# Six units by token halves behind each norm, weight remainders on GpSimd, and a later second layer, in a two-layer hybrid transformer

## The chip, the cores and the metric

The kernel runs on one core of a Trainium2 chip. A core has TensorE (PE) for matmuls, VectorE (DVE), ScalarE (ACT), GpSimd (POOL) and SyncE (SP); each runs its own instructions in a fixed order and waits for the others by semaphores. Matmuls write to PSUM, which has eight banks here. The metric is the device time of one launch in microseconds (us).

## The reference

Two layers over 512 tokens of width 1024, in fp32. Each layer has a mixer of four branches and a convolutional FFN, each between two RMS norms:

```python
for l in range(DEPTH):                       # 2
    h = rms_norm(x, norm_mix_pre[l])
    z = h @ w_in[l]
    za, zq, zkv, zg, zc, zd = jnp.split(z, offsets, axis=-1)
    y_conv = conformer_conv(za, ...)         # 31 taps per channel
    y_nsa = nsa_attention(q, kv..., gates, nsa_pe_k[l], nsa_pe_v[l],
                          nsa_ck_w1[l], nsa_ck_w2[l], nsa_cv_w1[l], nsa_cv_w2[l], cos, sin)
    y_sgu = spatial_gating(zc, ...)
    y_pool = multiscale_pool(zd, ...)
    y = jnp.concatenate([y_conv, y_nsa, y_sgu, y_pool], axis=-1) @ w_out[l]
    x = x + rms_norm(y, norm_mix_post[l])
    h = rms_norm(x, norm_ffn_pre[l])
    y = conv_ffn(h, ffn_up[l], ffn_conv_w[l], ffn_conv_b[l], ffn_down[l])   # 1024 -> 5632 -> 1024
    x = x + rms_norm(y, norm_ffn_post[l])

def compress(t, pe, w1, w2):                 # in nsa_attention, for keys and for values
    blocks = (t[:, blk_idx] + pe).reshape(bsz, n_cmp, CMP_LEN * HEAD_DIM)
    return jax.nn.gelu(blocks @ w1) @ w2     # first layer, gelu, second layer
```

## The kernel before, in words

Activations lie with channels on the 128 partitions and tokens along the free dimension (512, or two token halves of 256). A weight matrix is cut into units of 128 output columns, 92 per layer: four of NAT (tables that are wanted with tokens on the partitions), KK and CMP (keys, and what the compression reads), two of Q, four of CONV, two of SU (the spatial gating), two of the pooling branch, eight of the output projection, 44 of the FFN's up matrix (from `U_UP` = 24 on) and 24 of its down matrix (three phases of eight).

Each fp32 operand is split in a high part and a remainder, so a product is three matmuls per k-tile: hi x h's high part (`hh`), hi x h's remainder (`hl`), and lo x `hh` (lines L125 to L127). With eight k-tiles a unit is 24 matmuls of 512 columns, or 48 of 256 by token halves. `weights()` (L104 to L114) makes the two parts of a unit: a DMA loads `raw`, ACT copies it to `whi` (rounded to the matmul's type) and writes -`raw`, rounded alike, to `wlo`, and a DMA of POOL's queue reads the weight from HBM a second time and adds it to `wlo`, which leaves the remainder. `whi` and `wlo` have six buffers each, `raw` has two:

```python
nc.scalar.activation(hi[:, :cols], raw[:, :cols], AF.Copy)
nc.scalar.activation(lo[:, :cols], raw[:, :cols], AF.Copy, scale=-1.0)
nc.gpsimd.dma_start(lo[:, :cols], self.a["ws"][l, u, :, :cols], accum_op=OP.add)
```

The rows name these by line: L111 for the hi copy, L112 for the second copy, L113 for the accumulating DMA.

A norm seam works by token halves. `in_halves` computes the last six output tiles of a projection for half 0 and then for half 1, and after each half calls `post_norm`: a matmul with ones sums the squares over partitions (L212, the statistic), ACT takes the root (L213), DVE the reciprocal (L214, into `q` for half 0, `kh` for half 1, `rsx` for the next norm), `z` is scaled (L272), added to `x` by POOL or DVE (L99), and split again into `hh` (ACT, L246) and `hl` (DVE, L247), with squares (L236, L239) and a second statistic for the norm that follows, whose factor `rsx` is applied to the products afterwards. Statistics of half 0 have the PSUM bank "o", of half 1 bank "t" (two buffers, shared with the attention); products rotate through the five banks "mm" and "s". Behind a seam the first units are computed by halves, half 0 of all of them first, so that PE works while half 1 is normed: five up units in `ffn()`, four units (KK, CMP, two Q) in `mixer()`.

The mixer issues its steps from a list, `STEPS`. Among them "cmp" makes the compressed keys and values: the first layer (L497), a gelu on ACT (L502), and the second layer (L504, L510). The 31 taps of the convolution are DVE instructions (L609, L611); a rotary embedding swaps half of the rows by a DMA. In the FFN each up unit passes `conv3` (DVE L99, L809, ACT L806), pairs are gated (ACT L819) and split into `yh` and `yl` (L131, L99), and a phase's down units follow. The order on each engine is fixed when the program is built: a scheduler estimates times and places each instruction, so that a change in one part can move rows in another.

## Time and profile before

| | |
|---|---|
| time, median of 3 runs | 1229.5 us (1229.41 to 1232.96) |
| the profiled execution's time | 1228.64 us |
| its span, first to last instruction | 1226.7 us |
| mean granted TensorE clock | 0.971 |
| busy: PE, DVE, ACT, POOL | 1143.6, 663.1, 705.4, 336.1 us |
| HBM read | 192.79 MB |

Busy time counts an engine's instructions without its waits. The granted clock is a share of 2.4 GHz; 0.5 would be the lower level, 1.2 GHz. In the stretches, each engine has its busy time and its number of instructions, and then follow clock, DMA share and GB/s.

### The profile page before, as it was taken

Reading aid. Unit: us, or ns where it says so; the run is one execution under the profiler, and the core shown is the slowest. Engines: PE = TensorE matmul, PEld = TensorE weight load, DVE = VectorE, ACT = ScalarE, POOL = GpSimd, SP = SyncE. Lnnn points to the kernel's source line nnn. Section 1 sums busy time; section 2 is a strip of 40 time slices with the busy share of each in tenths; the row PEclk is TensorE's granted clock in tenths of the full one; section 3 lists DMA queues with packets and bytes.
Section 4 is the critical chain, followed back from the end, with each engine's and each line's share of the span. In section 5 each row is a group of like instructions: output and inputs, shape, how many; then the busy total and the mean of one; then the engine's idle time right before and its main releaser. Section 6 shows DMA issues by size and latency. Waiting matters only on the chain.

```text
span 1226.7 us, 16283 instructions
## 1 busy us (share of the span) xinstructions
PE 1143.6 (93%) x6168; PEld 956.0 (78%) x6168; DVE 663.1 (54%) x1065; ACT 705.4 (58%) x1094; POOL 336.1 (27%) x378
## 2 busy tenths in 40 slices
PE   6979899879999999999978899987999999999995
PEld 5868568878888888888976776877888888888895
DVE  5689951785125521544678998147550544134536
ACT  6558756567456544565464687554756664446541
POOL 2352642331111111111344545233212111111112
PEclk9989999889999999999989899997999999999998
DMA  8977514748799979887659391083879987889842
GB/s 233 244 174 161 117 52 104 172 119 182 167 238 205 187 182 195 189 186 157 149 123 217 75 205 36 1 202 74 199 154 231 225 187 172 205 186 189 183 96 68
DMA packets 64094, 197.53 MB, mean 161 GB/s; under 512 B 8720, under 2 KB 14864, under 8 KB 64016
## 3 DMA queue, kind: packets, MB, share of 16 engines
q0 software_dynamic: 26352, 92.91, 41.7%
q1 hardware_dynamic: 37664, 103.59, 28.4%
q8 instruction: 48, 0.79, 0.3%
...
HBM read 192.79 MB, written 2.10 MB: 159 GB/s over the span
## 4 chain that ended last, share of the span: by engine, by line
PE 73%; DVE 10%; DMA 6%; ACT 6%; issue 3%; SPq 1%; DVEq 0%; ACTq 0%; POOLq 0%
PE ps_s L126 13%; PE ps_s L127 13%; PE ps_s L125 13%; PE ps_mm L126 9%; PE ps_mm L127 9%; PE ps_mm L125 9%; DVE z L272 3%; DMA raw<-in_ws_dram 2%; DMA wlo<-in_ws_dram 2%; DVE z L611 2%; ACT wlo L112 1%; PE ps_o L742 1%; ACT whi L111 1%; PE ps_t L733 1%; DMA yh<-yh 1%
## 5 line engine op out<-in xcount | busy, mean ns | idle before, releaser
L113 POOL DMA_DIRECT2D wlo<-in_ws_dram x183 | 161.1, 883 | 716.4 <-ACT wlo L112 625.1
L111 ACT ACTIVATE whi<-raw 128x1024 fp32r<-128x1024 f32 (+2 forms) x183 | 188.4, 1030 | 249.1 <-PE ps_s L126 94.4
L126 PE MATMUL ps_s<-hl,whi 128*128 128x512 f32 (+1 forms) x552 | 202.8, 369 | 11.0 <-DVE hl L247 10.9
L125 PE MATMUL ps_s<-hh,whi 128*128 128x512 f32 (+1 forms) x552 | 200.9, 369 | 5.4 <-ACT hh L246 5.2
L127 PE MATMUL ps_s<-hh,wlo 128*128 128x512 f32 (+1 forms) x552 | 202.2, 368 | 2.5 <-DMA wlo<-in_ws_dram 2.5
L125 PE MATMUL ps_mm<-hh,whi 128*128 128x512 f32 (+1 forms) x488 | 184.8, 379 | 12.4 <-ACT hh L246 8.4
L126 PE MATMUL ps_mm<-hl,whi 128*128 128x512 f32 (+1 forms) x488 | 185.9, 381 | 10.9 <-DVE hl L247 10.5
L112 ACT ACTIVATE wlo<-raw 128x1024 fp32r<-128x1024 f32 (+2 forms) x183 | 186.3, 1018 | 0.7 <-PE ps_s L390 0.3
L127 PE MATMUL ps_mm<-hh,wlo 128*128 128x512 f32 (+1 forms) x488 | 184.2, 377 | 0.0
L126 PE MATMUL ps_s<-yl,whi 128*128 128x256 f32 (+1 forms) x406 | 134.9, 333 | 0.0
L127 PE MATMUL ps_s<-yh,wlo 128*128 128x256 f32 (+1 forms) x406 | 134.5, 332 | 0.2 <-DMA wlo<-in_ws_dram 0.2
L125 PE MATMUL ps_s<-yh,whi 128*128 128x256 f32 (+1 forms) x406 | 133.9, 334 | 0.4 <-ACT yh L131 0.3
L126 PEld LDWEIGHTS ps_s<-hl,whi 128*128 128x128 f32 x552 | 108.3, 197 | 29.7 <-DVE hl L247 12.2
L125 PEld LDWEIGHTS ps_s<-hh,whi 128*128 128x128 f32 x552 | 107.2, 197 | 23.6 <-ACT hh L246 5.6
L127 PEld LDWEIGHTS ps_s<-hh,wlo 128*128 128x128 f32 x552 | 108.0, 196 | 20.2 <-DMA wlo<-in_ws_dram 2.7
L125 PEld LDWEIGHTS ps_mm<-hh,whi 128*128 128x128 f32 x488 | 95.3, 195 | 30.7 <-ACT hh L246 9.0
L126 PEld LDWEIGHTS ps_mm<-hl,whi 128*128 128x128 f32 x488 | 95.0, 195 | 30.0 <-DVE hl L247 13.3
L127 PEld LDWEIGHTS ps_mm<-hh,wlo 128*128 128x128 f32 x488 | 95.1, 195 | 17.0
L809 DVE SCALAR_TENSOR_TENSOR q<-q,vec,q 128x511 f32<-128x511 f32 (+1 forms) x88 | 65.5, 750 | 57.3 <-ACT q L806 55.8
L127 PE MATMUL ps_mm<-yh,wlo 128*128 128x256 f32 (+1 forms) x266 | 87.5, 329 | 3.0 <-DMA wlo<-in_ws_dram 3.0
L125 PE MATMUL ps_mm<-yh,whi 128*128 128x256 f32 (+1 forms) x266 | 87.9, 331 | 0.0
L126 PE MATMUL ps_mm<-yl,whi 128*128 128x256 f32 (+1 forms) x266 | 87.4, 329 | 0.0
...
## 6 DMA issues: line engine op xcount, KB each, us to landing
raw<-in_ws_dram SPq DMA_DIRECT2D x159, 512.0 KB, 6.2
wlo<-in_ws_dram POOLq DMA_DIRECT2D x159, 512.0 KB, 7.6
...
```

Of the source, the lines that this page charges most:

```text
L111: nc.scalar.activation(hi[:, :cols], raw[:, :cols], AF.Copy)
L112: nc.scalar.activation(lo[:, :cols], raw[:, :cols], AF.Copy, scale=-1.0)
L113: nc.gpsimd.dma_start(lo[:, :cols], self.a["ws"][l, u, :, :cols], accum_op=OP.add)
L125: nc.tensor.matmul(ps, wh, ah, start=start and n == 0, stop=False)
L126: nc.tensor.matmul(ps, wh, al, start=False, stop=False)
L127: nc.tensor.matmul(ps, wl, ah, start=False, stop=stop and n == len(ks) - 1)
L272: nc.vector.scalar_tensor_tensor(t, t, gain(k), rs, op0=OP.mult, op1=OP.mult)
L611: nc.vector.scalar_tensor_tensor(acc[j], x, w, acc[j], op0=OP.mult, op1=OP.add)
L733: nc.tensor.transpose(pst[:, s * 128:(s + 1) * 128], P[s][:, kb * 128:(kb + 1) * 128], self.ident)
L742: nc.tensor.matmul(O[64 * c:64 * c + 64, :256], v, PT[:, 256 * c:256 * c + 256], start=b == 0 and kb == 0, stop=False, skip_group_check=True)
L809: nc.vector.scalar_tensor_tensor(t[:, s:], v[:, :S - s], fw(k), t[:, s:], op0=OP.mult, op1=OP.add)
```

## The change

It has four parts. (1) Six up units instead of five go by token halves behind a norm, and in the mixer six instead of four: `MORE` adds the two units of the first CONV step. (2) Where these are computed, and for all up units, products rotate through seven PSUM banks (the two of tag "t" join); the statistics of both halves share bank "o". (3) `on_dma(u)` decides how the remainder of a weight is made. Units below `U_UP + 10` keep ACT's second copy and the accumulating DMA, except CMP and Q at the start of the first layer; for these, and for the later 34 up and all 24 down units of each layer, POOL subtracts `whi` from `raw` in two column halves. (4) The second layer of the compression is a step of its own, "cmp2", behind the scores "a1".

```diff
--- before.py
+++ after.py
@@ -67,14 +67,16 @@
 
     LAST_POOL = (1, 4)
 
-    FIRST, FULL = 5, 2
+    FIRST, FULL = 6, 2
+
+    DMA_UPS, AT_START = 10, (U_KK, U_CMP, U_Q, U_Q + 1)
 
     FIRST_CUTS = ((0, 2), (2, 5), (5, 8))
 
     def __init__(self, tc, nc, a, cp, mp, wp, pp):
         self.tc, self.nc, self.a = tc, nc, a
         self.cp, self.mp, self.wp, self.pp = cp, mp, wp, pp
-        self.cyc = 0
+        self.cyc = self.l = 0
         self.fcyc = 0
 
 
@@ -90,16 +92,20 @@
         return self.pp.tile(list(shape), F, name="ps_" + tag, tag=tag,
                             bufs={"s": 3, "t": 2, "o": 1, "mm": 2}[tag])
 
-    def psr(self):
-        tag = ("mm", "s", "mm", "s", "s")[self.cyc % 5]
+    def psr(self, wide=False):
+        tags = ("mm", "s", "t", "mm", "s", "t", "s") if wide else ("mm", "s", "mm", "s", "s")
         self.cyc += 1
-        return self.ps(tag)
+        return self.ps(tags[self.cyc % len(tags)])
 
     def tt(self, out, x, y, op, eng=None):
         (eng or self.nc.vector).tensor_tensor(out, x, y, op=op)
 
     def eng(self, name):
         return self.nc.gpsimd if name in self.ON_POOL else self.nc.vector
+
+    def on_dma(self, u):
+
+        return u < U_UP + self.DMA_UPS and not (self.l == 0 and u in self.AT_START)
 
     def weights(self, l, u, cols=1024):
 
@@ -107,10 +113,16 @@
         raw = self.wp.tile([128, 1024], F, name="raw", tag="raw", bufs=self.RAW_BUFS)
         hi = self.wp.tile([128, 1024], R, name="whi", tag="whi", bufs=self.W_BUFS)
         lo = self.wp.tile([128, 1024], R, name="wlo", tag="wlo", bufs=self.W_BUFS)
-        nc.sync.dma_start(raw[:, :cols], self.a["ws"][l, u, :, :cols])
+        src = self.a["ws"][l, u, :, :cols]
+        nc.sync.dma_start(raw[:, :cols], src)
         nc.scalar.activation(hi[:, :cols], raw[:, :cols], AF.Copy)
-        nc.scalar.activation(lo[:, :cols], raw[:, :cols], AF.Copy, scale=-1.0)
-        nc.gpsimd.dma_start(lo[:, :cols], self.a["ws"][l, u, :, :cols], accum_op=OP.add)
+        if self.on_dma(u):
+            nc.scalar.activation(lo[:, :cols], raw[:, :cols], AF.Copy, scale=-1.0)
+            nc.gpsimd.dma_start(lo[:, :cols], src, accum_op=OP.add)
+        else:
+            n = cols // self.LO_CUT
+            for c in range(0, cols, n):
+                self.tt(lo[:, c:c + n], raw[:, c:c + n], hi[:, c:c + n].bitcast(F), OP.subtract, nc.gpsimd)
         return hi, lo
 
     def product(self, ps, w, ks, act, c0=0, c1=512, start=True, stop=True, kw=None):
@@ -217,7 +229,7 @@
 
         tags = (("q20", "q21", "q22", "q23"), ("kh0", "kh1", "kl0", "kl1"))[c]
         acc, rs = self.slot(tags[0]), self.slot(tags[1])
-        return {"c": slice(256 * c, 256 * c + 256), "tags": tags[2:], "n": 0, "pair": None, "ps": ("o", "t")[c],
+        return {"c": slice(256 * c, 256 * c + 256), "tags": tags[2:], "n": 0, "pair": None, "ps": "o",
                 "acc": [acc[:, :256], acc[:, 256:]], "rs": [rs[:, :256], rs[:, 256:]]}
 
     def pair(self, H):
@@ -339,7 +351,9 @@
     def first_weights(self, l):
         return [self.weights(l, u) for u in (U_KK, U_CMP, U_Q, U_Q + 1)]
 
-    STEPS = ("conv0", "consts", "conv1", "cmp", "kk", "q1", "nat", "w", "q0", "gates", "a1", "taps", "probs", "su",
+
+    MORE = (U_CONV + 2, U_CONV)
+    STEPS = ("conv0", "consts", "conv1", "cmp", "kk", "q1", "nat", "w", "q0", "gates", "a1", "cmp2", "taps", "probs", "su",
              "v", "pool0", "a0", "b0", "b1", "p0", "p1", "pool1", "a2", "b2", "fp", "p2", "a3", "b3", "p3", "fg",
              "others", "sum", "cn")
 
@@ -349,7 +363,9 @@
         h, rsx = self.h, self.rsx
 
         wk = self.first if l == 0 else self.first_weights(l)
-        psk, psc, *psq = pk = [self.psr() for _ in wk]
+        wk = wk + [self.weights(l, u) for u in self.MORE]
+        pk = [self.psr(True) for _ in wk]
+        psk, psc, psq, ahead = pk[0], pk[1], pk[2:4], dict(zip(self.MORE, pk[4:]))
         for c in range(2):
             for ps, w in zip(pk, wk):
                 self.product(ps[:, 256 * c:256 * c + 256], w, range(KT), h, 256 * c, 256 * c + 256)
@@ -359,6 +375,8 @@
         m = {}
 
         def proj(u):
+            if u in ahead:
+                return ahead[u]
             ps = self.ps("mm")
             self.product(ps, self.weights(l, u), range(KT), h)
             return ps
@@ -449,7 +467,8 @@
             m["pcT"] = self.compressed_probs(qc, m["gates"])
 
         steps = {
-            "consts": constants, "nat": nat, "gates": gates, "kk": keys, "cmp": lambda: self.compressed(l, psc), "probs": probs,
+            "consts": constants, "nat": nat, "gates": gates, "kk": keys, "cmp": lambda: m.update(g1=self.compressed(l, psc)),
+            "cmp2": lambda: self.compressed_out(m["g1"]), "probs": probs,
             "su": lambda: self.gating_u([proj(U_SU + j) for j in range(2)]),
             "v": lambda: self.gating_v(m["nat"]), "w": self.gating_w, "fg": lambda: self.gating_finish(m["nat"]),
             "taps": lambda: self.taps(gl, acc), "others": lambda: self.other_taps(gl),
@@ -500,6 +519,11 @@
         nc.vector.tensor_copy(g1, ps1[64:, :64])
         self.tt(g1, g1, ps1[:64, :64], OP.add)
         nc.scalar.activation(g1, g1, AF.Gelu_apprx_tanh)
+        return g1
+
+    def compressed_out(self, g1):
+
+        nc = self.nc
         ps2 = self.ps("o")
         nc.tensor.matmul(ps2[:, :32], self.w2[:, :128], g1[:, :32], start=True, stop=True)
         for p in (0, 64):
@@ -826,7 +850,7 @@
         self.new_z()
         first = self.FIRST
         ws = [self.weights(l, U_UP + m) for m in range(first)]
-        pss = [self.psr() for _ in range(first)]
+        pss = [self.psr(True) for _ in range(first)]
         for c in range(2):
             for m in range(first):
                 self.product(pss[m][:, c * 256:(c + 1) * 256], ws[m], range(KT), h, c * 256, (c + 1) * 256)
@@ -839,7 +863,7 @@
                     if m < first:
                         ps = pss[m]
                     else:
-                        ps = self.psr()
+                        ps = self.psr(True)
                         self.product(ps, self.weights(l, U_UP + m), range(KT), h)
                     p.append(ps)
                 finish(f, *p)
```

Order on POOL, start of the program, before. `q20` and `kh0` are sums of squares of the two token halves; `wlo_150` is CMP's remainder, `wlo_181` and `wlo_188` those of the two Q units, the next ones those of CONV units.

```order
L99 TENSOR_TENSOR q20_108<-q20_108,q22_206 128x256
L113 DMA wlo_150<-in_ws_dram 128x1024
L99 TENSOR_TENSOR kh0_110<-kh0_110,kl0_219 128x256
L113 DMA wlo_181<-in_ws_dram 128x1024
L99 TENSOR_TENSOR kh0_110<-kh0_110,kl0_229 128x256
L113 DMA wlo_188<-in_ws_dram 128x1024
L113 DMA wlo_455<-in_ws_dram 128x1024
L113 DMA wlo_491<-in_ws_dram 128x1024
```

And with the change (in its source the additions stand on L101, the accumulating DMA on L121):

```order
L101 TENSOR_TENSOR q20_108<-q20_108,q22_206 128x256
L101 TENSOR_TENSOR wlo_150<-raw_148,whi_149 128x512 x2
L101 TENSOR_TENSOR kh0_110<-kh0_110,kl0_219 128x256
L101 TENSOR_TENSOR wlo_181<-raw_179,whi_180 128x512 x2
L101 TENSOR_TENSOR wlo_188<-raw_186,whi_187 128x512 x2
L101 TENSOR_TENSOR kh0_110<-kh0_110,kl0_229 128x256
L121 DMA wlo_243<-in_ws_dram 128x1024
L121 DMA wlo_250<-in_ws_dram 128x1024
```

The three accumulating DMAs became three pairs of subtractions at about the same places, and the CONV units keep theirs.

Order on PE around the second compression layer, layer 0, before: L389 to L391 are the products of a NAT unit, and L504 is the second layer.

```order
L389 MATMUL ps_mm_787<-whi_736,hh2_94 128x396
L390 MATMUL ps_mm_787<-wlo_737,hh2_94 128x396
L391 MATMUL ps_mm_787<-whi_736,hl2_95 128x396
L504 MATMUL ps_o_682<-g1_678,w2_545 128x32
L389 MATMUL ps_mm_787<-whi_736,hh3_96 128x396
L390 MATMUL ps_mm_787<-wlo_737,hh3_96 128x396
L391 MATMUL ps_mm_787<-whi_736,hl3_97 128x396
```

And with the change, where L733 and L734 are attention scores, L736 adds the mask, and L528 is the second layer:

```order
L734 MATMUL ps_s_939<-kl0_555,q21_560 128x256
L733 MATMUL ps_s_939<-kh0_553,q23_562 128x256
L734 MATMUL ps_s_939<-kl0_555,q23_562 128x256
L736 LDWEIGHTS identb_76
L736 MATMUL ps_s_939<-maskb_77,identb_76 128x2x128
L528 MATMUL ps_o_954<-g1_726,w2_593 128x32
L733 MATMUL ps_s_1187<-kh0_553,q20_559 128x256
L734 MATMUL ps_s_1187<-kl0_555,q20_559 128x256
```

The second layer moved from the middle of a NAT unit to between two blocks of scores.

Order on PE at the norm ahead of the second FFN, before: L212 with `kh0` is the post-norm's statistic of half 1, the rows around it are half 0 of the up units.

```order
L127 MATMUL ps_mm_7476<-hh0_6833,wlo_7467 128x256
L126 MATMUL ps_s_7472<-hl5_6844,whi_7438 128x256
L127 MATMUL ps_s_7472<-hh5_6843,wlo_7439 128x256
L125 MATMUL ps_s_7472<-hh6_6845,whi_7438 128x256
L212 MATMUL ps_t_7371<-kh0_6853,ones_78 128x256
L126 MATMUL ps_s_7473<-hl5_6844,whi_7445 128x256
L127 MATMUL ps_s_7473<-hh5_6843,wlo_7446 128x256
L125 MATMUL ps_s_7473<-hh6_6845,whi_7445 128x256
L126 MATMUL ps_mm_7474<-hl5_6844,whi_7452 128x256
```

And with the change, where L137 to L139 are the three matmuls of a product and L224 is the statistic:

```order
L137 MATMUL ps_t_7604<-hh1_6955,whi_7593 128x256
L138 MATMUL ps_t_7604<-hl1_6956,whi_7593 128x256
L139 MATMUL ps_t_7604<-hh1_6955,wlo_7594 128x256
L137 MATMUL ps_t_7604<-hh2_6957,whi_7593 128x256
L224 MATMUL ps_o_7491<-kh0_6973,ones_78 128x256
L138 MATMUL ps_t_7604<-hl2_6958,whi_7593 128x256
L139 MATMUL ps_t_7604<-hh2_6957,wlo_7594 128x256
L137 MATMUL ps_t_7604<-hh3_6959,whi_7593 128x256
L138 MATMUL ps_t_7604<-hl3_6960,whi_7593 128x256
```

Before, 70 half-0 matmuls of the up units (of 120) stand ahead of the statistic; with the change 127 (of 144), and it goes to bank "o". At the norm ahead of the first FFN the counts are 97 and 127, ahead of the second mixer 66 and 99 (of 96 and 144).

Order on DVE at the same place, before: `kh1` is the factor of half 1's post-norm, `rsx` that of the next norm; the reciprocal of `rsx` stands ten rows further down, behind the scaling of `z`.

```order
L99 TENSOR_TENSOR q20_6851<-q20_6851,q22_7187 128x256
L214 RECIPROCAL kh1_6854<-kh1_6854 128x256
L272 SCALAR_TENSOR_TENSOR z0_6824<-z0_6824,vec_4736,kh1_6854 128x256
L272 SCALAR_TENSOR_TENSOR z1_6825<-z1_6825,vec_4736,kh1_6854 128x256
L272 SCALAR_TENSOR_TENSOR z2_6826<-z2_6826,vec_4736,kh1_6854 128x256
```

And with the change:

```order
L101 TENSOR_TENSOR q20_6971<-q20_6971,q22_7307 128x256
L226 RECIPROCAL rsx_6952<-rsx_6952 128x256
L226 RECIPROCAL kh1_6974<-kh1_6974 128x256
L284 SCALAR_TENSOR_TENSOR z0_6944<-z0_6944,vec_4808,kh1_6974 128x256
L284 SCALAR_TENSOR_TENSOR z1_6945<-z1_6945,vec_4808,kh1_6974 128x256
```

The reciprocal of `rsx` now stands ahead of that of `kh1`. At the other two norms before it stood directly behind `kh1`, and now it stands ahead of it there too.

## Rows read from the trace of the kernel before

**Rows 1.** The page, busy time of each engine: us, share of the span, instructions

```profile
PE 1143.6 (93%) x6168; PEld 956.0 (78%) x6168; DVE 663.1 (54%) x1065; ACT 705.4 (58%) x1094; POOL 336.1 (27%) x378
```

**Rows 2.** The waits of PE: us in total, times, longest us

```profile
PE ps_o L504 <- ACT g L502: 12.6, 2, 7.2
PE ps_s L126 <- DVE hl L247: 10.9, 4, 4.4
```

**Rows 3.** Engines by stretch (start:end in us); PEclk is the granted clock

```profile
80.00:90.00 10.00, 3.87 (x13) 3.81 (x14) 9.90 (x13) 4.69 (x7) 4.85 (x4) 0.66 0.50 122
110.00:120.00 10.00, 10.00 (x48) 8.17 (x47) 7.45 (x19) 9.91 (x18) 3.82 (x6) 1.00 0.93 202
150.00:160.00 10.00, 10.00 (x75) 6.14 (x75) 7.89 (x18) 7.09 (x18) 3.22 (x4) 1.00 0.05 15
280.00:300.00 20.00, 20.00 (x87) 16.06 (x86) 12.84 (x19) 14.31 (x21) 3.50 (x4) 1.00 0.86 188
```

**Rows 4.** The timeline of the start: start us, us, instruction, [idle before <-releaser]

```profile
14.87 1.01 POOL L113 DMA_DIRECT2D wlo<-in_ws_dram  x1 [1.82 <-ACT wlo L112]
23.86 0.39 PE L127 MATMUL ps_s<-hh,wlo 128*128 128x256 f32 x1 [2.53 <-DMA wlo<-in_ws_dram]
35.42 0.46 ACT L213 ACTIVATE rsx<-ps_t,eps 128x256 f32<-128x256 f32 x1
49.05 0.69 DVE L435 SCALAR_TENSOR_TENSOR yl<-ps_s,rsx 128x512 f32<-128x512 f32 x1 [4.62 <-PE ps_s L127]
68.97 0.69 DVE L99 TENSOR_TENSOR yh<-yh,sin 128x512 f32<-128x512 f32 x1 [3.58 <-DMA yh<-yh]
```

**Rows 5.** The timeline around the second compression layer, first layer of the model

```profile
76.25 5.51 DVE L611 SCALAR_TENSOR_TENSOR z<-z,vec,z 128x512 f32<-128x512 f32 x3
86.13 0.63 PE L504 MATMUL ps_o<-g,w 64*128 64x32 f32 x2 [7.22 <-ACT g L502]
```

**Rows 6.** The timeline of the norm ahead of the first FFN, PE and DVE

```profile
241.34 0.59 PE L212 MATMUL ps_t<-kh,ones 128*128 128x256 f32 x2
242.48 1.75 DVE L214 RECIPROCAL kh<-kh 128x256 f32<-128x256 f32 x1 [8.49 <-ACT kh L213]
```

**Rows 7.** The timeline of the norm ahead of the second mixer, PE and DVE

```profile
620.74 0.60 PE L212 MATMUL ps_t<-kh,ones 128*128 128x256 f32 x2
656.69 0.69 DVE L99 TENSOR_TENSOR yh<-yh,cos 128x512 f32<-128x512 f32 x1 [2.55 <-DMA yl<-yh]
659.36 0.79 DVE L99 TENSOR_TENSOR yh<-yh,sin 128x512 f32<-128x512 f32 x1 [1.37 <-DMA yh<-yl]
671.83 0.69 DVE L99 TENSOR_TENSOR yh<-yh,sin 128x512 f32<-128x512 f32 x1 [1.12 <-DMA yh<-yh]
```

**Rows 8.** The timeline of the norm ahead of the second FFN, PE and DVE

```profile
842.08 0.60 PE L212 MATMUL ps_t<-kh,ones 128*128 128x256 f32 x2
851.47 1.74 DVE L214 RECIPROCAL rsx<-rsx 128x256 f32<-128x256 f32 x1
```

**Rows 9.** The timeline of an FFN phase boundary: last up unit, first use

```profile
306.42 1.54 DVE L809 SCALAR_TENSOR_TENSOR kh<-kh,vec,kh 128x511 f32<-128x511 f32 x2 [1.48 <-ACT kh L806]
308.42 0.69 DVE L99 TENSOR_TENSOR kl<-ps_s,rsx 128x512 f32<-128x512 f32 x1 [0.45 <-PE ps_s L127]
313.86 0.69 DVE L99 TENSOR_TENSOR yl<-kh,yh 128x512 fp32r<-128x512 f32 x1 [0.70 <-ACT yh L131]
318.43 0.40 PE L125 MATMUL ps_mm<-yh,whi 128*128 128x512 f32 x1
```

**Rows 10.** Groups of instructions, POOL: xcount | busy us, mean ns | idle before

```profile
L99 POOL TENSOR_TENSOR yl<-yl,yl 128x512 f32<-128x512 f32 x8 | 16.4, 2048 | 11.1 <-ACT yl L624 11.1
L99 POOL TENSOR_TENSOR yl<-tmp,yh 128x512 fp32r<-128x512 f32 x4 | 5.1, 1286 | 4.0 <-ACT yh L131 4.0
```

**Rows 11.** The page, costliest groups: ACT, the hi copies

```profile
L111 ACT ACTIVATE whi<-raw 128x1024 fp32r<-128x1024 f32 (+2 forms) x183 | 188.4, 1030 | 249.1 <-PE ps_s L126 94.4
```

**Rows 12.** DMA issues, 330 to 560 us: xcount, KB, median us to landing

```profile
raw<-in_ws_dram SPq DMA_DIRECT2D x43, 512.0 KB, 7.3
```

## Prediction

> **What bounds the kernel now.** I read the page first, then the waits of PE, then each stretch by windows, and last the timeline at the seams. PE is busy for 93% of the span [rows 1], so at most 83 us of its idle time is to be had, plus what a lower clock costs after each gap. The windows say that the stretches differ. In an FFN stretch PE is busy 20.00 of 20 us with 87 matmuls, DVE only 12.84 and ACT 14.31 [rows 3]: nothing but fewer matmuls would help there. In the first mixer, at 80 to 90 us, DVE is busy 9.90 of 10 and PE 3.87, at a granted clock of 0.66 (the lower level, 1.2 GHz, for part of it, after PE had stood idle); at 110 to 120 DVE has 2.55 us free and PE is full; from 150 on PE is full and DVE is not [rows 3]. So the mixer begins bound by DVE and ends bound by PE: what starts DVE's chain earlier moves the end. The third kind of place is the seam at a norm, where PE waits for hl, 10.9 us in one row of its list [rows 2].
>
> My unit of work is the 512-column matmul: 20.00 / 87 = 0.230 us [rows 3]. A 256-column one is taken as half, 0.115, and a unit (24 matmuls) as 5.52 us, 2.76 per token half.
>
> **The start and the first mixer.** Before, CMP's lo is made by an accumulating DMA that POOL issues at 14.87; PE gets it at 23.86, after a wait of 2.53 [rows 4]. After, POOL computes it in two instructions of 128x512, which the trace shows at 1.286 us alone and 2.048 in the worst group [rows 10], so 2.6 to 4.1 us: ready at about 17.5 to 19, some 5 to 6 us earlier than 23.86. The same holds for Q and Q+1, whose pieces stand directly behind in POOL's queue. Queued behind these six instructions are one addition of squares and the accumulating DMAs of the two CONV units; both wait for loads that are still under way. CMP's matmuls are now interleaved with those of KK, so they fill the gaps in which PE waited for the split of h.
>
> What that is worth is read on DVE: it waits 4.62 us at 49.05 for the last matmul of Q+1, and 3.58 at 68.97 for the rotary swap, a DMA that follows on q0, hence on the CONV units and steps ahead of it [rows 4]. With the four units done early and two CONV units by halves in the gap, both waits go: 4.62 + 3.58 = 8.2 us. Bounds: 3 (the CONV units still come by accumulating DMA, and PE waits for them in place of Q+1) and 13 (8.2, plus the 2.55 us that DVE has free at 110 to 120 [rows 3], plus about 2 because ACT's square root at 35.42 [rows 4] no longer stands behind a late weight). I take **-8.2**, because the chain behind it is DVE's without a gap.
>
> **The second compression layer.** PE waits 7.22 us at 86.13 for the gelu [rows 5], 12.6 over both layers of the model [rows 2]. After, that matmul stands behind the scores of three blocks instead of amid the nat products, so this wait goes. But the gelu is late because DVE is: ahead of it three taps take 5.51 us, 1.84 each, and DVE is 99% busy there [rows 3, 5]. What waits next is PE for probabilities and DVE's other results. I count **0** alone; the bound is -12.6 for the two, if PE rather than DVE set the pace up to 150 us, which the windows deny.
>
> **The norm seams.** All statistics now use one bank, and the scheduler has put the post-norm statistic of token half 1 at the same place in all three seams, behind 127 of 144 half-0 matmuls (99 of 144 ahead of the second mixer). Before, it stood behind 97, 66 and 70. It runs at 241.34, 620.74 and 842.08 [rows 6, 7, 8], and everything of half 1 follows it. So half 1 starts later by 30, 33 and 57 matmuls: 3.5, 3.8 and 6.6 us. In return the reciprocal of rsx, 1.75 us, is done before this chain and not inside it (it stood inside at all three; for the last one at 851.47 [rows 8]): -1.75 each.
> - First FFN: +3.5 - 1.75, then the sixth unit's half 1 (+2.76) in place of the whole unit behind (-5.52): **-1.0**.
> - Second mixer: +3.8 - 1.75 + 2 x 2.76 - 2 x 5.52 = -3.5 on PE. On DVE, which sets the pace of the mixer, work begins 2.0 later, but its waits of 2.55, 1.37 and 1.12 [rows 7] can be filled with taps, since the CONV pair is done earlier: -5.0 + 2.0 = **-3.0**.
> - Second FFN: +6.6 - 1.75 + 2.76 - 5.52 = **+2.1**. This seam is the one that the change harms: only 17 matmuls, 2.0 us, are left to cover a chain at whose end PE already waits up to 4.4 us for hl [rows 2].
> Each could be off by 3 us: a longer gap lowers the clock, a shorter one spares that.
>
> **FFN weights.** Of each layer 58 units (34 up, 24 down) lose ACT's second copy and the accumulating DMA, and POOL gets two instructions per unit, at 1.286 to 2.048 us: 2.6 to 4.1 of the 5.52 us that PE needs for an up unit [rows 3, 10]. ACT's 116 copies at about 1.03 us (the like copy, [rows 11]) and some 58 MB of DMA go, worth **0**: PE is full there, and no wait of its list of more than 3 us names these weights. The cost could be on DVE, which reads two SBUF operands in most of its FFN instructions. The like trace: a scalar-tensor-tensor takes 0.77 us alone [rows 9], 1.84 beside POOL's additions [rows 5]. So one POOL instruction can cost DVE up to 1.07 us, two per unit 2.1; DVE's load of 64% [rows 3] rises to at most (3.5 + 2.1) / 5.52, 100%. Where it would show is the phase boundary: the last up product's chain begins on DVE at 308.42 and ends at 313.86 + 0.69 = 314.55, and PE first needs it at 318.43 [rows 9]: 3.9 us of cover. Two or three POOL instructions meet that chain of 6 us: 2 to 3.2 us, just hidden. So 0, at most +1.5 at each of six boundaries, +9.
>
> The Trainium skill, in "SBUF — State Buffer", section "Who interferes with whom", says that a DVE instruction with two SBUF inputs and a GpSimd instruction that reads SBUF exclude each other, and that the loser waits for the whole instruction. By that rule one meeting could cost DVE the full 1.29 us, and three at a boundary 3.9, exactly the cover, so the sum would stay, with nothing to spare; the trace's 1.84 against 0.77 agrees with it.
>
> **Sum.** -8.2 + 0 - 1.0 - 3.0 + 2.1 + 0 = -10.1. The profiled execution took 1228.64 (span 1226.7); 1218.5 by that. The median of the runs shown is 0.9 above it: **1219 us**, which is 0.8% faster.
>
> **Rivals.**
> 1. *The seams and new waits eat it (same).* The mixer gives only its lower bound, 3, since PE waits for the CONV units' accumulating DMA instead; the seams sum to +1, not -1.9. 1229.5 - 2: 1227.5. For it: the later statistic stands in the program. Against: DVE's 8.2 us of waits have named causes that the change removes.
> 2. *DVE and POOL exclude each other in the FFN (slower).* With 2 POOL instructions per unit, DVE falls behind and y's last piece comes 3.9 us late or more. It decides from the fourth collision within one boundary's chain on: at 1.07 to 1.29 us each, seven of them (one for each DVE instruction of the chain) would be 7.5 to 9 less 3.9, some 4 to 5 us; at six boundaries +24 to +30, with the rest 1243 to 1249. Two such late boundaries would already undo the gain. Against it: at 1.286 us each, POOL's two fill less than half of a unit's 5.52 us.
> 3. *The loads become the bound (slower).* A raw buffer is now held until POOL has read it: landing 7.3 [rows 12], the hi copy 1.03 [rows 11], POOL 2.6 to 4.1; over two buffers (10.9 to 12.4) / 2 = 5.5 to 6.2 us, against 5.52. At the worst 0.7 x 116 = 81 us more. Against it: 7.3 was measured beside the accumulating DMAs, which are gone for these units, and half the bytes go with them; the loads decide from a landing of 6 us on, with POOL at its slowest.
> 4. *More than the sum.* PE in the mixers is spared its gaps and the lower clock too: the upper bound of the start (-13), and in the second mixer a full -5 with the stall of 5.4 us gone in part: -22, 1207.
>
> **How the numbers follow.** I give the forecast (1211 to 1225) 0.53, rival 1 0.15, rivals 2 and 3 0.07 and 0.04, rival 4 0.21. Less than 0.3% (3.7 us) is about what a measurement of this kernel cannot tell from none. Faster: the forecast and rival 4, 0.74. Same: 0.15. Slower: 0.11. Leaving out rivals 2 and 3 above and the far end of rival 4 below gives 1203 to 1229.
>
> **What would show it.** Right, step by step: POOL's subtractions for CMP between 15 and 19 us and no PE wait for its lo; DVE's wait of 4.62 near 49 gone and mixer stretches that end some 8 us earlier; no wait for the gelu; the half-1 statistic behind most of half 0 and, at the second FFN, a longer PE wait for hl; FFN stretches with PE still full at 87 matmuls in 20 us. Wrong: PE gaps at the phase boundaries with DVE instructions of 1.3 us and more, PE waits for wlo or whi inside the FFN, or a new wait of DVE in the first mixer as long as those removed.

## The result and the profile after

The changed kernel takes 1248.1 us (median of 4 runs, 1243.7 to 1248.8) against 1229.5 of the kernel before (4 runs): ratio 1.0133, interval 1.0100 to 1.0166. The forecast was 1219 with a range of 1203 to 1229, so both the direction and the range were wrong. The profiled execution took 1248.8 us, span 1247.0, clock 0.960 (before 0.971).

The busy times of the engines, to compare with [rows 1]: PE did the same work, DVE got 93 us busier, ACT 110 less busy, POOL 235 busier.

```profile
PE 1146.6 (92%) x6312; PEld 963.4 (77%) x6312; DVE 755.9 (61%) x1065; ACT 595.4 (48%) x973; POOL 570.6 (46%) x497
```

To see where the 20.3 us of span went, I cut the span at PE's own work: the first product of the output projection (its operand is yh), the first product of the up units behind it (operand hh), the first down product (yh again), and so on. Each number is the difference of two start times in PE's timeline of the profiled execution, in us; "first phase" is the seam with the first 12 up units, "downs" the eight down units behind it. The rest of the FFN was the same in both (269.9 us in the first layer, 224.5 in the second), and so was the end.

| kernel | mixer 1 | projection | first phase | downs | mixer 2 | projection | first phase | downs |
|---|---|---|---|---|---|---|---|---|
| before | 164.6 | 58.9 | 84.7 | 33.4 | 153.4 | 63.4 | 80.1 | 33.4 |
| changed | 171.9 | 61.3 | 85.7 | 34.5 | 155.8 | 60.3 | 87.0 | 36.0 |
| second layer put back (e1) | 152.8 | 61.6 | 84.9 | 34.3 | 155.7 | 63.9 | 83.2 | 35.6 |
| start only (e6) | 156.5 | 59.5 | 83.8 | 33.4 | 156.0 | 57.2 | 82.7 | 33.4 |
| halves only, one statistics bank (e7) | 163.7 | 60.8 | 85.1 | 33.4 | 156.3 | 64.5 | 85.6 | 33.4 |
| halves only, two statistics banks (e13) | 164.8 | 58.5 | 82.1 | 33.4 | 151.9 | 65.2 | 77.0 | 33.4 |
| changed, second layer back, two statistics banks (e16) | 159.4 | 61.2 | 76.8 | 34.7 | 151.0 | 63.2 | 77.5 | 34.9 |

The first two rows are the result; the others belong to the experiments. A row is one execution, and a stage can differ by some us from one to the next: e1's is the fastest of ten (1228.4 us), e13's the slowest of six (1222.8), e16's the slowest of five (1215.2). The first mixer lost 7.3 where 8.2 was to be won, and the second seam with its first phase lost 6.9.

The windows of the changed kernel, in the form of [rows 3]:

```profile
80.00:90.00 10.00, 6.66 (x43) 5.99 (x41) 10.00 (x13) 1.50 (x3) 9.17 (x3) 1.00 0.00 0
110.00:120.00 10.00, 10.00 (x47) 7.91 (x46) 6.49 (x20) 9.92 (x21) 4.43 (x6) 1.00 0.91 204
150.00:160.00 10.00, 9.44 (x74) 6.54 (x75) 9.89 (x23) 7.44 (x20) 2.75 (x4) 1.00 0.06 15
280.00:300.00 20.00, 20.00 (x109) 17.11 (x109) 15.13 (x19) 14.54 (x18) 10.03 (x8) 1.00 0.78 205
920.00:940.00 20.00, 17.63 (x76) 13.99 (x75) 13.28 (x15) 7.17 (x11) 8.60 (x8) 1.00 0.25 79
```

At 80 to 90 DVE is busy for all 10 us, and now POOL too, for 9.17 us with three instructions. That is the row to stop at: POOL's instructions of this kind took 1.3 to 2 us [rows 10]. At 280 to 300 the FFN is as full as before; at 920 to 940 PE lost 2.4 us; before, no wait of PE was to be seen in the FFN behind the first phase of up units. The timeline of the first of these places, one row each of DVE, POOL, ACT and PE:

```profile
82.72 13.99 DVE L635 SCALAR_TENSOR_TENSOR z<-z,vec,z 128x512 f32<-128x512 f32 x21
83.54 14.29 POOL L101 TENSOR_TENSOR yl<-yl,yl 128x512 f32<-128x512 f32 x1 [0.83 <-ACT yl L648]
97.87 0.72 ACT L648 ACTIVATE yl<-z,vec 128x512 f32<-128x512 f32 x1 [14.40 <-POOL yl L101]
99.12 0.58 PE L733 MATMUL ps_s<-kh,q 128*128 128x256 f32 x1 [12.46 <-ACT nat L410]
```

Read it from the top. DVE runs 21 taps in 13.99 us, 0.67 each and without a gap. POOL's addition, which begins 0.8 us behind the first of them, ends only at 97.83, after the run. ACT needs the buffer that this addition reads and waits 14.40 us with everything queued behind it, among it the copies to nat. PE waits 12.46 us for that. Before, the longest wait at this point of the program was that for the gelu, 7.22 us [rows 5].

The start, to compare with [rows 4]:

```profile
13.35 2.71 POOL L101 TENSOR_TENSOR wlo<-raw,whi 128x512 fp32r<-128x512 f32 x2 [0.51 <-ACT whi L118]
30.86 0.46 ACT L225 ACTIVATE rsx<-ps_o,eps 128x256 f32<-128x256 f32 x1
39.22 0.58 PE L139 MATMUL ps_t<-hh,wlo 128*128 128x256 f32 x1 [0.92 <-DMA wlo<-in_ws_dram]
45.99 0.69 DVE L101 TENSOR_TENSOR yh<-yh,cos 128x512 f32<-128x512 f32 x1 [4.82 <-DMA yl<-yh]
63.61 0.69 DVE L101 TENSOR_TENSOR yh<-yh,sin 128x512 f32<-128x512 f32 x1 [2.50 <-DMA yh<-yh]
```

POOL makes CMP's remainder in 2.71 us and has it at 16.06; PE's wait of 2.53 for it is gone, and ACT takes the root of half 1 at 30.86 instead of 35.42. DVE still waits 4.82 and 2.50 us, both times for a rotary swap (before, the first of these waits was for PE), and 3.1 and 5.4 us earlier. Last, PE's list of waits, its statistics of half 1 (at the last seam half 0's pre-norm statistic too), and the FFN:

```profile
PE ps_s L138 <- DVE hl L259: 20.6, 8, 5.3
PE ps_s L137 <- ACT hh L258: 13.2, 6, 5.5
PE ps_s L733 <- ACT nat L410: 12.5, 1, 12.5
```

The first row does not say that the wait for hl doubled against [rows 2]. Before, it stood in two rows, 10.9 us there and 10.5 here, and its sum, 21.4, is now 20.6:

```profile
PE ps_mm L126 <- DVE hl L247: 10.5, 6, 4.5
```

```profile
255.65 0.60 PE L224 MATMUL ps_o<-kh,ones 128*128 128x256 f32 x2
637.64 0.59 PE L224 MATMUL ps_o<-kh,ones 128*128 128x256 f32 x2
859.71 0.60 PE L224 MATMUL ps_o<-q,ones 128*128 128x256 f32 x2
863.11 0.60 PE L224 MATMUL ps_o<-kh,ones 128*128 128x256 f32 x2
873.44 0.58 PE L138 MATMUL ps_s<-hl,whi 128*128 128x256 f32 x1 [4.03 <-DVE hl L259]
```

```profile
L833 DVE SCALAR_TENSOR_TENSOR q<-q,vec,q 128x511 f32<-128x511 f32 (+1 forms) x88 | 110.9, 1265 | 42.2 <-ACT q L830 40.8
L101 POOL TENSOR_TENSOR wlo<-raw,whi 128x512 fp32r<-128x512 f32 (+1 forms) x238 | 331.7, 1417 | 296.6 <-ACT whi L118 296.3
```

```profile
938.30 0.50 PE L137 MATMUL ps_mm<-yh,whi 128*128 128x512 f32 x1 [2.37 <-ACT yh L143]
```

The statistics of half 1 run at 255.65, 637.64 and 863.11 (241.34, 620.74 and 842.08 in [rows 6, 7, 8]). At 859.71 stands the pre-norm statistic of half 0, which now must come first. The FFN's DVE instructions take 1265 ns on average instead of the 0.77 us of [rows 9], and at the end of the first phase PE waits for y's last piece, 2.37 us at 938.30 and 0.84 at 329.30.

### The profile page after: what moved, and what is told of

Read it like the earlier page. It is cut to its first block, busy times and chain, and to the rows that moved or that the text cites. A ratio compares the mean times of both kernels' runs of the same rounds, so it can differ in the third digit from the quotient of the medians.

```text
span 1247.0 us, 16471 instructions
## 1 busy us (share of the span) xinstructions
PE 1146.6 (92%) x6312; PEld 963.4 (77%) x6312; DVE 755.9 (61%) x1065; ACT 595.4 (48%) x973; POOL 570.6 (46%) x497
## 3 DMA queue, kind: packets, MB, share of 16 engines
q0 software_dynamic: 9216, 32.61, 14.3%
## 4 chain that ended last, share of the span: by engine, by line
PE 60%; DVE 18%; DMA 10%; ACT 6%; issue 2%; POOL 2%; SPq 1%; DVEq 0%; ACTq 0%; POOLq 0%
PE ps_s L138 10%; PE ps_s L139 10%; PE ps_s L137 10%; PE ps_mm L137 6%; PE ps_mm L139 6%; PE ps_mm L138 6%; DMA raw<-in_ws_dram 6%; DVE z L635 4%; DVE z L284 3%; PE ps_t L139 3%; PE ps_t L138 3%; PE ps_t L137 3%; DMA wlo<-in_ws_dram 2%; DVE q L833 2%; ACT wlo L120 2%
## 5 line engine op out<-in xcount | busy, mean ns | idle before, releaser
L101 POOL TENSOR_TENSOR wlo<-raw,whi 128x512 fp32r<-128x512 f32 (+1 forms) x238 | 331.7, 1417 | 296.6 <-ACT whi L118 296.3
L138 PE MATMUL ps_s<-hl,whi 128*128 128x512 f32 (+1 forms) x464 | 167.8, 362 | 20.7 <-DVE hl L259 20.6
L137 PE MATMUL ps_s<-hh,whi 128*128 128x512 f32 (+1 forms) x464 | 166.0, 359 | 13.2 <-ACT hh L258 13.2
L139 PE MATMUL ps_s<-hh,wlo 128*128 128x512 f32 (+1 forms) x464 | 165.4, 357 | 1.1 <-DMA wlo<-in_ws_dram 1.1
L121 POOL DMA_DIRECT2D wlo<-in_ws_dram x64 | 55.6, 869 | 201.8 <-ACT wlo L120 147.7
L137 PE MATMUL ps_mm<-hh,whi 128*128 128x512 f32 (+1 forms) x352 | 135.7, 385 | 5.2 <-DVE bs L604 2.4
L833 DVE SCALAR_TENSOR_TENSOR q<-q,vec,q 128x511 f32<-128x511 f32 (+1 forms) x88 | 110.9, 1265 | 42.2 <-ACT q L830 40.8
L137 PE MATMUL ps_s<-yh,whi 128*128 128x256 f32 (+1 forms) x406 | 133.5, 331 | 3.1 <-ACT whi L118 3.1
L139 PE MATMUL ps_s<-yh,wlo 128*128 128x256 f32 (+1 forms) x406 | 133.9, 330 | 1.5 <-DMA wlo<-in_ws_dram 1.5
L139 PE MATMUL ps_mm<-hh,wlo 128*128 128x512 f32 (+1 forms) x352 | 134.7, 383 | 0.0
L138 PE MATMUL ps_mm<-hl,whi 128*128 128x512 f32 (+1 forms) x352 | 134.6, 382 | 0.0
L137 PEld LDWEIGHTS ps_s<-hh,whi 128*128 128x128 f32 x464 | 91.6, 197 | 26.9 <-ACT hh L258 14.5
L139 PEld LDWEIGHTS ps_s<-hh,wlo 128*128 128x128 f32 x464 | 91.2, 196 | 14.1 <-DMA wlo<-in_ws_dram 1.5
L137 PE MATMUL ps_t<-hh,whi 128*128 128x512 f32 (+1 forms) x272 | 95.9, 353 | 0.2
L139 PE MATMUL ps_t<-hh,wlo 128*128 128x512 f32 (+1 forms) x272 | 94.9, 349 | 1.2 <-DMA wlo<-in_ws_dram 1.2
L138 PE MATMUL ps_t<-hl,whi 128*128 128x512 f32 (+1 forms) x272 | 95.8, 352 | 0.0
L137 PE MATMUL ps_mm<-yh,whi 128*128 128x256 f32 (+1 forms) x266 | 88.9, 334 | 3.2 <-ACT yh L143 3.2
L139 PE MATMUL ps_mm<-yh,wlo 128*128 128x256 f32 (+1 forms) x266 | 87.8, 330 | 1.0 <-DMA wlo<-in_ws_dram 1.0
```

What stands on the lines that cost most here:

```text
L101: (eng or self.nc.vector).tensor_tensor(out, x, y, op=op)
L121: nc.gpsimd.dma_start(lo[:, :cols], src, accum_op=OP.add)
L137: nc.tensor.matmul(ps, wh, ah, start=start and n == 0, stop=False)
L138: nc.tensor.matmul(ps, wh, al, start=False, stop=False)
L139: nc.tensor.matmul(ps, wl, ah, start=False, stop=stop and n == len(ks) - 1)
L833: nc.vector.scalar_tensor_tensor(t[:, s:], v[:, :S - s], fw(k), t[:, s:], op0=OP.mult, op1=OP.add)
```

## The experiments

Theory S: the moved second layer leaves DVE with 21 taps in a row, POOL is shut out for the whole run, and ACT and PE queue up behind it. Theory L: the loss lies in the seams, the FFN and late weights. Later theory B joined them: one statistics bank is what makes the halves dear. Times are medians; a ratio is against the kernel before, measured beside it, with its interval.

**e1_no_cmp2: the second layer put back.**

```diff
-    STEPS = (... "a1", "cmp2", "taps", ...)
+    STEPS = (... "a1", "taps", ...)
-            "cmp": lambda: m.update(g1=self.compressed(l, psc)),
-            "cmp2": lambda: self.compressed_out(m["g1"]),
+            "cmp": lambda: self.compressed_out(self.compressed(l, psc)),
```

> The changed kernel with the second compression layer back in its old step; the rest of the change stays. Theory S (21 taps in a row on DVE shut POOL out for 14 us, ACT and then PE wait behind POOL's addition): DVE's runs are now 5, 7 and 9 taps with copies between them, POOL's longest addition falls from 14.3 to 4 us or less, PE's wait of 12.5 for the copy to nat goes, though a wait of some 5 us for the gelu comes back; the first mixer ends 8 to 14 us earlier, total 1232 to 1240. Theory L (the loss lies in the seams, the FFN and late weights): the move costs nothing, total 1246 to 1249.

1232.6, ratio 1.0015 (0.9996 to 1.0034): 15.5 us less than the changed kernel, as theory S says. POOL's longest addition, and DVE beside it:

```profile
77.77 3.71 POOL L101 TENSOR_TENSOR yl<-yl,yl 128x512 f32<-128x512 f32 x1 [0.83 <-ACT yl L647]
76.94 3.38 DVE L634 SCALAR_TENSOR_TENSOR z<-z,vec,z 128x512 f32<-128x512 f32 x5
80.25 0.38 DVE L529 COPY kcbd<-ps_o 64x32 f32<-64x32 f32 x2
```

Five taps, then a copy of the second layer's result from PSUM to kcbd, then seven more. POOL's addition began at 77.77, right behind the first of the five, and ended at 81.48, that is 1.2 us behind the start of this copy: the copy let it in. (In the changed kernel the addition ended 1.2 us behind the start of the first DVE instruction behind the 21 taps.) The first mixer became 19.1 us shorter (171.9 to 152.8), but not all of that belongs to this step: e8 below runs the same instructions in the same order there, and took 157.4. From the start of POOL's long addition to the end of the mixer it is 88.3 us in the changed kernel, 75.0 in e1 and 74.6 in e8, so the step itself gives 13 to 14 us, about ACT's wait of 14.4. PE's wait for the gelu came back (10.4 us in total) without harm.

**e2_cmp2_only: the kernel before with the second layer moved.** The diff is the part of the change on STEPS, "cmp2" and compressed_out alone.

> The kernel before with only the second compression layer moved behind the scores a1. DVE then has 21 taps in a row in both layers. Theory S: an addition of POOL takes 10 us or more in one layer or in both, PE waits for nat behind it, total 1236 to 1250. Theory L: the gelu wait goes (12.6 us of PE time, of which little is on DVE's chain), total 1225 to 1230.

1244.8, ratio 1.0123 (1.0092 to 1.0154). The move by itself costs 15 us. POOL is shut out once in each layer:

```profile
85.69 14.29 POOL L99 TENSOR_TENSOR yl<-yl,yl 128x512 f32<-128x512 f32 x1 [0.83 <-ACT yl L630]
692.54 14.28 POOL L99 TENSOR_TENSOR yl<-yl,yl 128x512 f32<-128x512 f32 x1 [0.84 <-ACT yl L630]
```

How it reaches the end differs. In the first layer most is regained by the end of the FFN's first phase (mixer +3.0, projection +8.1, first phase -10.3); in the second the mixer loses 12.8.

**e3_adds_dve: the victim taken away.**

```diff
-                    self.tt(other[j], other[j], t, OP.add, nc.gpsimd)
+                    self.tt(other[j], other[j], t, OP.add)
```

> The changed kernel with the additions of the last five taps on DVE instead of POOL (eight instructions per layer, 0.7 us each, 5.5 us more DVE work in each mixer). Theory S: no instruction of POOL is left to be shut out there, ACT does not wait 14 us for a buffer; 1236 to 1244 in spite of the added DVE work. Theory L: 5 to 11 us more, 1253 to 1259.

1233.9, ratio 1.0042 (1.0024 to 1.0061): with eight more additions per layer on DVE the kernel is 14 us faster than the changed one. Below the range expected, on the side of theory S.

**e5_breaks: the run broken.** All of the change, and one column copied on DVE after every fourth tap:

```diff
                     nc.vector.scalar_tensor_tensor(acc[j], x, w, acc[j], op0=OP.mult, op1=OP.add)
+                    if j == 1 and k % 2:
+                        nc.vector.tensor_copy(self.slot("brk", F, (128, 1)), acc[j][:, :1])
```

> The whole changed kernel, with one copy of a single column (one input in SBUF) added on DVE after every fourth tap, so that the longest run of taps is 5 instead of 21; it adds 13 small instructions of some 0.1 us per layer and no result uses them. If POOL is shut out by the unbroken run of DVE instructions with two inputs in SBUF, its longest addition falls from 14.3 to under 5 us and the total to 1230 to 1236, although the second layer stays where the change put it. If the place of the second layer itself is at fault (late copies to kcbd and vcbd, another order on PE), the total stays at 1244 to 1249.

1233.3, ratio 1.0026 (1.0011 to 1.0041). The second layer stays where the change put it, and adding instructions to the engine that is full gains 15 us: 12 of them in the first mixer (171.9 to 159.7), and 2.8 in FFN stretches that the copies do not touch, as the last section tells. POOL's longest addition there:

```profile
81.77 3.76 POOL L101 TENSOR_TENSOR yl<-yl,yl 128x512 f32<-128x512 f32 x1 [0.83 <-ACT yl L650]
```

A run of taps does not shut POOL out every time. In the changed kernel, the first two rows are the tap beside which the addition of 14.29 us began, at 83.54, and a tap of the second layer with 13 more behind it; then follow the addition that began beside that one, and the next tap:

```profile
83.38 0.73 DVE L635 SCALAR_TENSOR_TENSOR z<-z,vec,z 128x512 f32<-128x512 f32 x1
703.29 0.75 DVE L635 SCALAR_TENSOR_TENSOR z<-z,vec,z 128x512 f32<-128x512 f32 x1
703.54 1.64 POOL L101 TENSOR_TENSOR yl<-yl,yl 128x512 f32<-128x512 f32 x1 [0.83 <-ACT yl L648]
703.96 1.76 DVE L635 SCALAR_TENSOR_TENSOR z<-z,vec,z 128x512 f32<-128x512 f32 x1
```

This one came in after one tap, and it was DVE that waited. The first had begun 0.16 us after the start of its tap, this one 0.25 us. Over all traces of this case, of the additions that began inside a tap with three or more taps to follow, 14 of the 16 that began at most 0.17 us after its start took 3.7 us or more, and all 20 that began 0.25 to 0.37 us after it took 1.5 to 1.7. So beside a long run it matters, by these traces, where in a tap the addition begins; why is not shown.

**e4_all_dma: no remainder on POOL.** `on_dma` returns True always.

> The changed kernel with all remainders of weights by ACT's second copy and the accumulating DMA, as before; halves, banks and the moved layer stay (DVE has 20 taps in a row in the first layer). If POOL's subtractions slow the FFN's DVE work (theory F): DVE's L833 falls from 1.27 to 0.75 us, the two waits for y's last piece at the ends of the first phases go, total 3 to 5 us less from the FFN; the first mixer starts later by 6 to 8 us but POOL's long addition stays. Theory S alone: about 1245 to 1253. If the subtractions were the main loss: 1230 or less.

1254.0, ratio 1.0200 (1.0163 to 1.0237), 1 us above what theory S alone was to give. POOL's long addition is there, beside 20 taps:

```profile
87.26 14.85 POOL L101 TENSOR_TENSOR yh<-yh,yh 128x512 f32<-128x512 f32 x1 [2.45 <-ACT yh L648]
```

The first mixer ends 8.2 us later (180.1 against 171.9), and the downs are back at 33.4. So the start's subtractions are worth 8, those of the FFN cost.

**e6_start_only and e8_no_ffn_pool: the subtractions apart.** e6 is the kernel before with CMP's and Q's remainders on POOL. e8 is e1 with the FFN's remainders by DMA again:

```diff
-        return u < U_UP + self.DMA_UPS and not (self.l == 0 and u in self.AT_START)
+        return not (self.l == 0 and u in self.AT_START)
```

> The kernel before with one part of the change: at the start POOL makes the remainders of CMP and the two Q units. If the term of the prediction for the start holds, the first mixer's end moves by 6 to 10 us, total 1220 to 1224. If that gain in the changed kernel came from the two CONV units by halves instead, 1226 to 1230.

1219.5, ratio 0.9920 (0.9900 to 0.9940): the start alone gives 10 us, 8.1 of it in the first mixer. DVE's first wait did not go, though; it came 3.3 us sooner, for a rotary swap instead of PE. The second came 7.8 us sooner and shrank from 3.58 to 1.07 us:

```profile
45.80 0.69 DVE L101 TENSOR_TENSOR yh<-yh,cos 128x512 f32<-128x512 f32 x1 [5.00 <-DMA yh<-yl]
61.18 0.69 DVE L101 TENSOR_TENSOR yh<-yh,sin 128x512 f32<-128x512 f32 x1 [1.07 <-DMA yh<-yh]
```

> The changed kernel with the second layer in its old place and, besides, no subtraction on POOL in the FFN (those of the start stay). If POOL's subtractions are what makes PE wait at the end of the first FFN phase, the stretch of its down units goes back from 34.3 and 35.7 us to 33.4 in both layers, and the total is 3 to 5 us under that of the kernel with only the second layer put back. If these waits come from six units by halves, nothing changes.

1229.9, ratio 0.9995 (0.9978 to 1.0013); the downs behind the first phases are 33.4 in both layers, where e1 has 34.3 and 35.6, and the two waits for y's last piece are gone. The total is 2.7 under e1, with intervals that overlap; the place is shown by the stages, the sum only about. The FFN's DVE instructions beside accumulating DMAs:

```profile
L832 DVE SCALAR_TENSOR_TENSOR q<-q,vec,q 128x511 f32<-128x511 f32 (+1 forms) x88 | 65.7, 750 | 60.1 <-ACT q L829 58.5
```

**e7, e9, e10, e11: the halves and the bank.** All with remainders by DMA and the second layer in its old place. e7 is the kernel before with six units, seven banks and one statistics bank; e9 has `FIRST = 5`, e10 has `MORE = ()`, e11 both.

> The kernel before with the other part: six units by halves behind each norm, seven banks, all statistics in one bank; remainders by DMA, second layer in its old place. If the later statistic of half 1 costs what the seams of the changed kernel showed (about +2 in the second mixer, +3 at the seam behind it, 0 at the first), total 1233 to 1237. By the prediction's terms it would be 1225 to 1229.

> The kernel before with six units by halves in the mixer alone (both layers), seven banks and one statistics bank; five up units in the FFN, remainders by DMA, second layer in its old place. If the cost of the halves comes from the single statistics bank (theory B: half 1's statistic then stands behind half 0 of nearly everything at each seam), total 1235 to 1241, like the kernel with all halves. If it comes from the six up units, 1228 to 1232.

> The kernel before with six up units by halves in the FFN alone, seven banks and one statistics bank; the mixer has its four units. Theory B: 1235 to 1241 here too. If the two CONV units in the mixer make the cost, 1228 to 1232.

> The kernel before with seven banks for products and one bank for the statistics, but four and five units by halves as before; the statistic of half 1 then stands behind 120 of 120, 96 of 96 and 120 of 120 half-0 matmuls. Theory B: nearly the whole cost is there without any sixth unit, 1235 to 1240. If more units by halves are the cost, 1228 to 1231.

e7: 1241.0, ratio 1.0095 (1.0076 to 1.0114). e9: 1247.6, 1.0141 (1.0118 to 1.0163). e10: 1233.3, 1.0027 (1.0007 to 1.0047). e11: 1235.7, 1.0047 (1.0027 to 1.0068). The bank alone costs 5, the halves with it from 3 to 17, and the whole less than one part: they do not add up. Only e11 lies in the range of theory B; e10 lies between the ranges, e7 and e9 above them all. In e9 the statistic stands behind all 120 half-0 matmuls of the FFN's units, and PE waits there 4.4 and 3.5 to 3.7 us, but so it stands in e11; what e9 loses besides lies in the second mixer and the projection behind it (158.8 and 66.7 us, before 153.4 and 63.4). I did not find out why.

**e13_own_bank: the statistic of half 1 with its own bank.** Six units as in e7:

```diff
-        tags = ("mm", "s", "t", "mm", "s", "t", "s") if wide else ("mm", "s", "mm", "s", "s")
+        tags = ("mm", "s", "t", "mm", "s", "s") if wide else ("mm", "s", "mm", "s", "s")
-        return {..., "ps": "o",
+        return {..., "ps": ("o", "t")[c],
-        self.stats(H["ps"], H["acc"][1], ...)      # pre_norm
+        self.stats("o", H["acc"][1], ...)
```

> The kernel before with six units by halves, but the post-norm statistic of half 1 keeps a bank of tag t (products rotate through six banks); the pre-norm statistics use bank o. The statistic of half 1 then stands behind 90, 66 and 70 half-0 matmuls again, not behind 127, 99 and 127. Theory B (the single statistics bank, by the late place of that statistic, makes the cost of the halves): 1227 to 1232, against 1241 for the same kernel with one bank. If six units by halves are dear of themselves, 1237 to 1243.

1218.7, ratio 0.9911 (0.9890 to 0.9931), 22 us less than e7: better than theory B expected. At the second FFN's seam, the wait for hl before; e7's statistic of half 1, its waits for hh and hl, and a window behind (PE busy with its count, clock):

```profile
853.56 0.39 PE L126 MATMUL ps_s<-hl,whi 128*128 128x256 f32 x1 [3.97 <-DVE hl L247]
856.13 0.59 PE L224 MATMUL ps_o<-kh,ones 128*128 128x256 f32 x2
861.11 0.40 PE L137 MATMUL ps_s<-hh,whi 128*128 128x256 f32 x1 [2.39 <-ACT hh L258]
866.45 0.58 PE L138 MATMUL ps_s<-hl,whi 128*128 128x256 f32 x1 [4.09 <-DVE hl L259]
865.00:870.00 5.00, 3.55 (x16) 0.50 0.00 0
```

And the same places with the statistic in its own bank:

```profile
840.76 0.59 PE L224 MATMUL ps_t<-kh,ones 128*128 128x256 f32 x2
852.26 0.39 PE L138 MATMUL ps_mm<-hl,whi 128*128 128x256 f32 x1 [1.09 <-DVE hl L259]
850.00:855.00 5.00, 3.91 (x33) 1.00 0.00 0
```

From the statistic to the first matmul with hl it is 10.3 us in e7, and 11.5 in e13 and before: the chain itself is no longer in e7, even a little shorter. But in e13 74 half-0 matmuls still lie behind the statistic, and PE is busy for all but 1.1 us of the wait; in e7 17 are left, PE waits 2.4 and 4.1 us, and its clock falls to 0.50, the lower level. Over this first phase PE stands idle 12.2 us in e7 and 7.1 in e13, at a mean clock of 0.88 and 0.96, and the phase takes 85.6 and 77.0 us. e13 changes two things, the statistic's bank and with it the number of banks for products (six, not seven); no run tells them apart.

**e12 and e14: the copies alone.** e12 is e6 with the breaks of e5, e14 the kernel before with them.

> The kernel before with POOL's remainders at the start only and the short copies between the taps (runs of at most 5; before: 9 with an addition of POOL of 3.7 us). If POOL's being shut out costs time in the kernel before as well, 1214 to 1218; if not, 1219 to 1222, the same as with the start alone or a little more for the added copies.

> The kernel before with the short copies between the taps and nothing else. If POOL's being shut out (a 3.7 us addition, runs of 9) costs time in the kernel before: 1224 to 1228. If the gain that the copies gave beside the start came from another order at the norms (there the statistic of half 1 moved), 1229 to 1232.

e12: 1215.5, ratio 0.9880 (0.9858 to 0.9902). e14: 1227.1, ratio 0.9982 (0.9967 to 0.9997). Both totals lie in the range that was expected if POOL's being shut out costs time there too, but the stages do not bear it out. In the kernel before POOL is shut out for 3.7 us at most, and breaking that shows no gain in the mixers: e14's are 166.9 and 154.4 us (before 164.6 and 153.4), e12's first is 161.2 (e6 156.5). So the right number is no sign that POOL's being let in gave e12's gain over e6; where it came from is told last, in part.

**e15 and e16: the parts joined.** e15 is e13 with the start on POOL and the breaks. e16 is the changed kernel with two things undone: the second layer as in e1, the banks as in e13.

> Six units by halves with the statistic of half 1 in its own bank, POOL's remainders at the start only, and the short copies between the taps; second layer in its old place. If the parts add up (start -11, copies -4, halves about 0): 1212 to 1218. If the halves still cost, 1220 to 1228.

> The changed kernel with two things undone: the second layer is back in its old step, and the post-norm statistic of half 1 has a bank of tag t of its own (six banks for products). POOL's subtractions in the FFN and at the start stay, and six units by halves. If these two explain the miss, it keeps the start's gain (-11) and the halves' with their own bank (-11) and loses some 3 in the FFN: 1210 to 1217. If something else of the change costs, 1222 or more.

e15: 1210.6, ratio 0.9841 (0.9820 to 0.9862). e16: 1209.2, ratio 0.9831 (0.9805 to 0.9858), 39 us under the changed kernel and 1.7% under the one before; both are about 1 us under the ranges expected if the parts add up. These two things, the place of the second layer and the banks, explain the miss. The busy times of e16, where PE reaches 94% of the span:

```profile
PE 1140.3 (94%) x6312; PEld 956.0 (79%) x6312; DVE 753.9 (62%) x1065; ACT 600.9 (50%) x976; POOL 563.9 (46%) x497
```

## Why the prediction was wrong

The parts, measured apart, come to about the whole: -11 for the start (e6), +15.5 for the second layer (e1), +10 for the halves with one statistics bank (e7) and +3 for POOL in the FFN (e1 against e8) make +17.5; the changed kernel is 18.7 above the one before. One row of the profile before belongs to the second point:

```profile
89.03 3.71 POOL L99 TENSOR_TENSOR yl<-yl,yl 128x512 f32<-128x512 f32 x1 [0.83 <-ACT yl L624]
```

- **The start, forecast -8.2: right by the number.** e6 gives 10 to 11 us, and all that the change did there shows. The way was in part another: of DVE's two waits the first stayed (4.62, in e6 5.00 us), only the second shrank, and DVE's reciprocal behind ACT's root of half 1 came 5.0 us earlier (30.94 instead of 35.91), which the prediction had in its upper bound alone, at about 2.
- **The second layer, forecast 0 with a gain as the only bound: this step failed, by 15 us.** I asked what the wait for the gelu was worth, and that was answered rightly: it came back in e1 and the mixer ended no later for it. I did not ask what else went with the layer. Its results are copied out of PSUM by DVE, and these copies stood between the taps; with them gone DVE had 21 two-input instructions in a row, and POOL's addition waited for the end of the run. The row that warned was there: POOL's additions of 2048 ns on average [rows 10] held this one of 3.71 us, and I read the average as a price. I used the exclusion of DVE and POOL only where DVE would be the loser (rival 2), and in the FFN, not in the mixer.
- **The seams, forecast -1.9 together: this step failed too, by 12 to 14 us.** e7 measures +10 to +12. The forecast is a sum of two things: the units by halves, -2.76 at each FFN and -5.0 in the second mixer, -10.5 together; and half 1's later start less the reciprocal, +1.75, +2.0 and +4.85, +8.6 together. With a bank of its own for the statistic, which then comes no later (behind 90, 66 and 70 half-0 matmuls), the same six units gain 11 us by the medians (e13), about the -10.5; its stages show -2.6 and -3.1 in the first phases but only -1.5 in the second mixer, so that share came out by number only. So the mis-sized term is the later statistic: 8.6 forecast, some 21 measured (e7 against e13, which differ by one product bank too). Its places were right: counted from half 0's post-norm statistic (at 223.64, 609.74 and 831.08; before 213.37, 598.10 and 817.39) that of half 1 comes 4.0, 5.3 and 7.3 us later (forecast 3.5, 3.8 and 6.6). The credit for the reciprocal came in the main: from this statistic to the first matmul with hl it is 10.3 to 10.4 us at each seam, before 11.5 to 11.7, so 1.2 to 1.4 of the 1.75.
- **What failed in that term is to price a delay by its length alone.** The matmuls that moved ahead of the statistic had been the cover of the wait behind it. At the first FFN 17 half-0 matmuls are left behind the statistic, 23 before, and the first phase is 0.4 us longer in e7; at the second 17 are left, 50 before, two bare waits stand where there was one, PE comes out of them at half clock, and the phase is 5.5 longer. In the second mixer 45 are left, 30 before, so it is not the cover: there DVE's waits were to be filled with taps, and were not (3.14, 1.68 and 1.26 us in the changed kernel, 2.55, 1.37 and 1.12 before), and the mixer is 2.9 longer in e7. The rest of e7's loss stands in the two projections (+1.9 and +1.1), and its cause is open. I also read the late place as the scheduler's choice. With one bank the order is forced: half 0's pre-norm statistic (859.71) must be read out by ACT's root before half 1's post-norm statistic (863.11) can be written.
- **The FFN, forecast 0 and at most +9: about right,** some 3 us, and at the place named: the end of the first phase, where y's last piece comes late; over the whole FFN a DVE instruction of that kind takes 1265 ns instead of 750. It was so at the first phase of each layer alone, not at all six boundaries.
- **The Trainium skill** ("SBUF — State Buffer", section "Who interferes with whom") says that of a DVE instruction with two SBUF inputs and a GpSimd instruction that reads SBUF one waits for the whole of the other. The runs agree, and go further: POOL's addition waited until the end of a run of 21 of DVE's, 14.3 us, and was let in by a copy that reads PSUM (e1) and by one of a single column (e5).
